# Layer-1 modulation of a two-layer diffusion trunk: from TensorE matmuls to sums on VectorE, ScalarE and GpSimd

## Chip, core and metric

One core of one Trainium2 chip. The metric is the device time of one execution of the whole program in microseconds, as the median of several runs.

## What is computed

A trunk of two layers over 256 latent tokens (x) and 256 context tokens (ctx), width 2048, in float32. Layer 0 runs neighbourhood attention (8 heads) beside latent attention (8 heads); layer 1 is a gated DeltaNet over both token sets. Each layer is steered by a modulation, and that is what the change is about:

```python
def adaln_params(cond, w_mod, b_mod):
    return jnp.split(jax.nn.silu(cond) @ w_mod + b_mod, 3, axis=-1)      # shift, scale, gate
def modulate(x, gain, shift, scale):
    return rmsnorm(x, gain) * (1 + scale) + shift
...
sh, sc, gt = adaln_params(c, w_mod, b_mod)              # for x
sh_c, sc_c, gt_c = adaln_params(c_ctx, w_mod, b_mod)    # for ctx
hx = modulate(x, norm, sh, sc) @ w_in
hc = modulate(ctx, norm, sh_c, sc_c) @ w_in
...
x = x + gt * y
if update_ctx:                                          # layer 0 only
    ctx = ctx + gt_c * y_c
```

For each layer two vectors of 2048 (one for x, one for ctx, the two "samples" of the change) go through a 2048 x 6144 matrix. The last layer does not update ctx, so its gate for ctx is never used.

## The kernel before

All activations lie feature-major: 128 features on the partitions, the 512 tokens (256 of x, 256 of ctx) along the free dimension. A dense product takes a weight tile of 128 x 1024, which ScalarE casts to a high part (whi, line 77) and VectorE completes with a low part (wlo = raw - whi, line 78); TensorE then runs three 128x512 matmuls per contraction tile (lines 90 to 92) into one of two mm tiles in PSUM. Weights come through SP's DMA queue into four raw buffers, whi and wlo have three buffers each.

The 6144 outputs of a modulation are cut into 12 chunks of 512: chunks 0 to 3 are the shift, 4 to 7 the scale, 8 to 11 the gate. A chunk reads 16 contraction tiles of 128x512, two to an mraw buffer (three buffers). There are two ways to compute one:

- `adaln` (TensorE, line 127): sixteen matmuls of four column groups into a PSUM tile pmod, a copy macc (line 133), four transposes pmt (line 136), and a reduction into the tile mod (line 138).
- `adaln_lanes` (lines 147 to 179): for each of the 16 contraction tiles and each of the two samples, VectorE adds tile times condition to a running sum lacc (lines 161 and 163), 32 instructions a chunk. Eight short matmuls pml with a column of ones (line 170) then sum over the partitions.

Both are generators; the work around them calls `steps` to take some steps of the one at hand, and a scheduler, which orders the instructions of every engine by its own estimate of time, settles the final order. Every engine runs its queue strictly in that order. The stages that matter:

- the first stage (layer 0's input products, with layer 0's shift and scale by `adaln`);
- the neighbourhood heads 0 to 6 (tiles qT, kT, vT, sp, pr, PT, po). Beside them run, as lanes, chunks 8 to 11 of layer 0 and chunks 0 and 1 of layer 1;
- the latent ranks (craw), head 7, the rope queries qr, and the latent heads, whose weights are ab_wb. Beside them run chunks 2, 3 and 8, and at the end chunk 9 of layer 1 by `adaln` on TensorE;
- the gated outputs gh and gl (lines 480 and 481), and the output projection (weights ab_wo), sixteen units, each closed by x1A and x1B (line 493). Beside them run chunks 4 to 7 of layer 1 as lanes;
- the turn into layer 1: the norm (ss, rs, dg, rb, lines 190 to 199), `modulate` (mh on VectorE, line 221; hh on ScalarE, line 222; hl on GpSimd, line 229, or on VectorE, line 224), and layer 1's first products. Here chunks 10 and 11 run by `adaln`;
- layer 1: keys, queries, inverses (GpSimd: rhs, line 711), then the scans and the output.

The attention of a head goes sp (TensorE) to mx (VectorE, line 372) to pr (ScalarE's exponential, line 375) to rc and pr again (VectorE, lines 377 and 378) to pt (TensorE) to PT (ScalarE line 340, VectorE line 341) to po (TensorE) to goA and goB (VectorE, line 388). goB of a head marks its end; the stretches of the prediction are cut at such instructions.

## Time and profile before

| | |
|---|---|
| median of 3 runs | 2585.1 us (2583.42 to 2586.82) |
| span of the profiled execution, first to last instruction | 2580.0 us |
| mean granted TensorE clock | 0.985 |
| TensorE busy | 97% |
| VectorE / ScalarE / GpSimd busy | 72% / 44% / 10% |
| bytes moved | 394.30 MB, 153 GB/s on average |

The profiled execution's own time is its span of 2580.0 us; the median of the timed runs is 5.1 us more, and the sums are made on the span. The profile calls TensorE PE (PEld is its weight load), VectorE DVE, ScalarE ACT, GpSimd POOL and SyncE SP. In a row of busy time by stage stand the stretch in us from the start, its length, the busy time and instruction count of each engine, the granted clock, the share of the DMA engines and GB/s; the same table for one tile or one line counts that tile's or line's instructions only. In a row of a tile stand minimum, median and maximum duration in ns, then the first and last start. In a row of the timeline stand start, duration, engine, line, operation, out<-in, shape, count, and in brackets idle time before it and what ended it. In a row of a group stand busy us, mean ns and idle time before. A matmul record lasts 0.39 us while the next one starts after 0.23 us.

### The profile page before, as it was taken

How to read it: one execution, taken by the hardware profiler on the slowest of the kernel's cores; microseconds unless marked ns; L12 is line 12 of the kernel's file. 1: busy time of each engine (PE TensorE's matmuls, PEld its weight loads, DVE VectorE, ACT ScalarE, POOL GpSimd, SP SyncE). 2: the span in 40 equal slices, each digit the busy share in tenths (PEclk: the TensorE clock that was granted, in tenths of full speed). 3: DMA queues.
4: the chain of work that ended last, by engine and by line, in shares of the span. 5: the costliest groups of instructions: out<-in, count | busy, mean ns of one | idle time of the engine just before them, and what ended most of it. 6: DMA issues, size and time to landing. Idle time of an engine off the chain costs nothing.

```text
span 2580.0 us, 43446 instructions
## 1 busy us (share of the span) xinstructions
PE 2499.2 (97%) x16586; PEld 2039.0 (79%) x16586; DVE 1852.2 (72%) x3543; ACT 1146.6 (44%) x2484; POOL 267.4 (10%) x261
## 2 busy tenths in 40 slices
PE   6999999999999999989999999999999999999998
PEld 4657888888767788768888889897777777777898
DVE  4544788773455687758999999987677777777754
ACT  4223323232333422377656655643444445445353
POOL 0000000000000000133212222310000000003000
PEclk9999999999999999999999999999999999999999
DMA  8872655532343376644454544563333433335454
GB/s 258 289 247 90 201 172 167 175 114 96 117 153 100 120 230 221 212 139 157 142 156 152 160 138 150 159 213 100 88 99 115 119 99 106 113 91 174 153 188 140
DMA packets 201810, 394.30 MB, mean 153 GB/s; under 512 B 68225, under 2 KB 109697, under 8 KB 201473
## 3 DMA queue, kind: packets, MB, share of 16 engines
q1 hardware_dynamic: 200448, 389.98, 47.9%
q8 instruction: 131, 2.15, 0.4%
q10 hardware_dynamic: 1152, 1.54, 0.2%
q14 instruction: 79, 0.64, 0.1%
HBM read 356.28 MB, written 35.13 MB: 152 GB/s over the span
## 4 chain that ended last, share of the span: by engine, by line
PE 79%; DVE 9%; issue 6%; DMA 3%; ACT 2%; SPq 0%; POOL 0%; DVEq 0%; POOLq 0%; ACTq 0%
PE mm L90 19%; PE mm L91 18%; PE mm L92 18%; PE pks L982 3%; PE pmod L127 3%; DVE wlo L78 2%; PE sp L348 2%; PE ptr L994 2%; DVE X L770 1%; DVE outer L768 1%; PE po L348 1%; PE pu L798 1%; DVE acc L561 1%; PE ptr L1027 1%; PE psu L1013 1%
## 5 line engine op out<-in xcount | busy, mean ns | idle before, releaser
L90 PE MATMUL mm<-hh,whi 128*128 128x512 f32 (+1 forms) x2784 | 988.5, 355 | 3.7 <-ACT t L636 2.2
L92 PE MATMUL mm<-hh,wlo 128*128 128x512 f32 (+1 forms) x2784 | 962.2, 346 | 8.7 <-DVE wlo L78 7.5
L91 PE MATMUL mm<-hl,whi 128*128 128x512 f32 (+1 forms) x2784 | 963.2, 346 | 0.0
L77 ACT CAST whi<-raw 128x1024 fp32r<-128x1024 f32 (+2 forms) x346 | 338.3, 979 | 668.4 <-PE mm L91 515.6
L90 PEld LDWEIGHTS mm<-hh,whi 128*128 128x128 f32 x2784 | 535.7, 192 | 113.8 <-issue 32.6
L92 PEld LDWEIGHTS mm<-hh,wlo 128*128 128x128 f32 x2784 | 535.4, 192 | 73.1 <-DVE wlo L78 9.4
L91 PEld LDWEIGHTS mm<-hl,whi 128*128 128x128 f32 x2784 | 536.0, 193 | 62.2 <-issue 8.4
L78 DVE TENSOR_TENSOR wlo<-raw,whi 128x1024 fp32r<-128x1024 f32 (+2 forms) x346 | 402.7, 1166 | 212.9 <-ACT whi L77 206.1
L163 DVE SCALAR_TENSOR_TENSOR lacc<-mraw,cond,lacc 128x512 f32<-128x512 f32 x300 | 208.8, 749 | 0.0
L561 DVE SCALAR_TENSOR_TENSOR acc<-cin,taps,acc 128x508 f32<-128x508 f32 (+3 forms) x256 | 196.1, 767 | 6.7 <-ACT acc L552 4.3
L1004 DVE SCALAR_TENSOR_TENSOR vl<-ptr,egm,vh 128x128 fp32r<-128x128 f32 x224 | 64.6, 346 | 98.3 <-ACT rf L1001 39.4
L711 POOL TENSOR_TENSOR rhs<-ghl,incl 128x512 fp32r<-128x512 f32 (+1 forms) x96 | 108.4, 1139 | 133.4 <-PE pd L713 114.2
L127 PE MATMUL pmod<-mraw,cond 128*32 128x512 f32 (+2 forms) x640 | 94.3, 501 | 23.2 <-DMA mraw<-ab_wm 18.6
L768 DVE SCALAR_TENSOR_TENSOR outer<-L,bv,X 128x31 f32<-128x31 f32 (+15 forms) x248 | 112.4, 453 | 4.7
L1088 DVE TENSOR_TENSOR wlo<-raw,whi 128x1024 fp32r<-128x1024 f32 x84 | 102.6, 1222 | 14.4 <-ACT whi L1080 13.8
L194 POOL TENSOR_TENSOR rs<-ms,half 128x4 f32<-128x4 f32 (+1 forms) x5 | 4.7, 947 | 985.1 <-DVE ms L192 985.1
L770 DVE TENSOR_TENSOR X<-X,outer 128x31 f32<-128x31 f32 (+15 forms) x248 | 101.7, 410 | 4.6
L575 ACT ACTIVATE ac<-acc 128x128 f32<-128x128 f32 x160 | 37.4, 300 | 146.0 <-DVE acc L561 146.0
L90 PE MATMUL mm<-gh,whi 128*128 128x512 f32 x256 | 99.9, 392 | 1.7 <-DVE x1B L493 1.7
L91 PE MATMUL mm<-gl,whi 128*128 128x512 f32 x256 | 99.9, 390 | 0.2 <-DVE gl L481 0.2
L92 PE MATMUL mm<-gh,wlo 128*128 128x512 f32 x256 | 99.7, 390 | 0.0
L998 ACT ACTIVATE vh<-ptr,egm 128x128 fp32r<-128x128 f32 x224 | 71.0, 373 | 56.6 <-PE ptr L994 54.6
(289 smaller groups left out, 3629.2 us busy)
## 6 DMA issues: line engine op xcount, KB each, us to landing
raw<-dn_w SPq DMA_DIRECT2D x194, 512.0 KB, 4.0
mraw<-dn_wm SPq DMA_DIRECT2D x96, 512.0 KB, 4.7
mraw<-ab_wm SPq DMA_DIRECT2D x88, 512.0 KB, 5.4
raw<-ab_w SPq DMA_DIRECT2D x66, 512.0 KB, 3.8
raw<-dn_wo SPq DMA_DIRECT2D x64, 512.0 KB, 3.7
raw<-ab_wo SPq DMA_DIRECT2D x32, 512.0 KB, 4.6
raw<-ab_w SPq DMA_DIRECT2D x32, 256.0 KB, 3.6
spt<-sp SPq DMA_DIRECT2D x64, 128.0 KB, 2.8
```

What stands on the lines that cost most here:

```text
L77: A.copy(hi[:, :m], raw[:, :m])
L78: V.tensor_tensor(lo[:, :m], raw[:, :m], hi[:, :m].bitcast(F32), op=ALU.subtract)
L90: PE.matmul(ps, wh[:, c], xh[:, k0 + k, sl], start=first and k == 0, stop=False)
L91: PE.matmul(ps, wh[:, c], xl[:, k0 + k, sl], start=False, stop=False)
L92: end = PE.matmul(ps, wl[:, c], xh[:, k0 + k, sl], start=False, stop=last and k == kt - 1)
L127: PE.matmul(pmod[32 * q:32 * q + 32, :m], cond[:, 4 * kg + q, :], raw[c // 1024][:, half + c % 1024:half + c % 1024 + m], start=kg == 0, s ...
L163: V.scalar_tensor_tensor(acc[:, s], raw[:, q], cond[:, k, s:s + 1], acc[:, s], op0=ALU.mult, op1=ALU.add)
L561: V.scalar_tensor_tensor(o3[:, :, i0:i1], p3[:, :, i0 + d:i1 + d], taps[:, ch, t:t + 1], o3[:, :, i0:i1], op0=ALU.mult, op1=ALU.add)
L711: P.tensor_tensor(rhs, ghl[i].bitcast(F32)[:, d, kh * 8:kh * 8 + 2 * n].unsqueeze(2).broadcast_to(sh), incl[:, c].unsqueeze(1).broadcast_t ...
L768: V.scalar_tensor_tensor(o, L[:, rows, k:k + 1].broadcast_to([128, n, m]), bv[:, k:k + 1], X[:, k:k + 1, cols].broadcast_to([128, n, m]), ...
L770: V.tensor_tensor(X[:, rows, cols], X[:, rows, cols], o, op=ALU.subtract)
L1088: V.tensor_tensor(w, raws[j], h.bitcast(F32), op=ALU.subtract)
```

## The change

After the first stage no chunk is computed by `adaln`: every later chunk goes through `adaln_lanes`, and that is rewritten.

- The sum of sample 0 stays on VectorE (16 instructions a chunk). For sample 1, ScalarE multiplies the tile by the condition, in place in the mraw buffer (after VectorE has read it), and GpSimd adds it to a second running sum. The first of them is written by ScalarE directly.
- The last four chunks of layer 1 (8 to 11, the gate) are made for sample 0 alone: `ns` is 1, VectorE takes the even contraction tiles, ScalarE and GpSimd the odd ones, and the closing matmuls add the two running sums.
- Chunks 2, 3 and 8 are stepped three at a time in the latent heads; chunk 9 leaves the end of the latent heads and chunks 10 and 11 leave the turn; 9, 10 and 11 follow 4 to 7 beside the output projection, two steps at a time.

```diff
     def adaln_lanes(l, ps, pm, tp, chunks, after=None):
         for ch in chunks:
-            acc = tp.tile([128, 2, 512], F32, name="lacc", tag="lacc", bufs=1)
+            ns = 1 if l == 1 and ch >= 8 else 2
+            acc = [tp.tile([128, 512], F32, name=f"lacc{i}", tag=f"lacc{i}", bufs=1) for i in range(2)]
...
-                        for s in range(2):
-                            if k == 0:
-                                V.tensor_scalar(acc[:, s], raw[:, q], cond[:, k, s:s + 1], None, op0=ALU.mult)
+                        for e in range(2):
+                            if ns == 1 and e != k % 2:
+                                continue
+                            c = cond[:, k, e * (ns - 1):e * (ns - 1) + 1]
+                            if e == 0 and k == 0:
+                                V.tensor_scalar(acc[e], raw[:, q], c, None, op0=ALU.mult)
+                            elif e == 0:
+                                V.scalar_tensor_tensor(acc[e], raw[:, q], c, acc[e], op0=ALU.mult, op1=ALU.add)
+                            elif k <= 2 - ns:
+                                A.activation(acc[e], raw[:, q], AF.Copy, scale=c)
                             else:
-                                V.scalar_tensor_tensor(acc[:, s], raw[:, q], cond[:, k, s:s + 1], acc[:, s],
-                                                       op0=ALU.mult, op1=ALU.add)
+                                A.activation(raw[:, q], raw[:, q], AF.Copy, scale=c)
+                                P.tensor_tensor(acc[e], acc[e], raw[:, q], op=ALU.add)
...
-                for s in range(2):
-                    PE.matmul(pt[:, j, s:s + 1], acc[:, s, j * 128:j * 128 + 128], ones[:, 0:1], start=True, stop=True)
+                for e in range(2):
+                    s = e * (ns - 1)
+                    PE.matmul(pt[:, j, s:s + 1], acc[e][:, j * 128:j * 128 + 128], ones[:, 0:1],
+                              start=ns == 2 or e == 0, stop=ns == 2 or e == 1)
...
-        ahead, pace = later(mr, ((0, range(8, 12), 1), (1, (0, 1), 1))), 1
+        ahead, pace = later(mr, ((0, range(8, 12)), (1, (0, 1)))), 1
...
-        ahead = later(mr, ((1, (2, 3, 8), 0),))
+        ahead = later(mr, ((1, (2, 3, 8)),))
...
-            steps(ahead, 1)
+            steps(ahead, 3)
...
-        steps(later(mr, ((1, (9,), 0),), last_mm))
...
-                ahead, pace = later(mr, ((1, (4, 5, 6, 7), 1),), last_mm), 1
+                ahead, pace = later(mr, ((1, (4, 5, 6, 7, 9, 10, 11)),), last_mm), 2
...
-        ahead = later(mr, ((1, (10, 11), 0),), last_mm)
...
-        steps(ahead)
```

How the scheduler then orders the engines, at the places of which the prediction speaks. First VectorE in the latent heads, the third head as its stream stands before: attention alone (vt, mx, PT, qT, kT), the reciprocal rc and the low parts wlo of the weights.

```order
L344 SCALAR_TENSOR_TENSOR qT<-mm,qT 128x512
L377 RECIPROCAL rc<-sm 128x1
L378 TENSOR_SCALAR pr<-pr,rc 128x256
L78 TENSOR_TENSOR wlo<-raw,whi 128x512
L341 TENSOR_TENSOR kT<-mm,kT 128x512
L341 TENSOR_TENSOR PT<-pt,PT 128x4x128
```

The same place now (line numbers of the changed kernel; lacc_7517 is VectorE's running sum of chunk 4):

```order
L352 SCALAR_TENSOR_TENSOR qT<-mm,qT 128x512
L386 TENSOR_SCALAR pr<-pr,rc 128x256
L78 TENSOR_TENSOR wlo<-raw,whi 128x512
L166 TENSOR_SCALAR lacc_7517<-mraw,cond 128x512
L349 TENSOR_TENSOR kT<-mm,kT 128x512
L184 TENSOR_TENSOR mod_84<-pml,vecs 128x4
L168 SCALAR_TENSOR_TENSOR lacc_7517<-mraw,cond,lacc_7517 128x512
L349 TENSOR_TENSOR PT<-pt,PT 128x4x128
L385 RECIPROCAL rc<-sm 128x1
L168 SCALAR_TENSOR_TENSOR lacc_7517<-mraw,cond,lacc_7517 128x512
L386 TENSOR_SCALAR pr<-pr,rc 128x256
L168 SCALAR_TENSOR_TENSOR lacc_7517<-mraw,cond,lacc_7517 128x512
```

Chunk 4, which ran beside the output projection, now stands among the latent heads. Between the end of head 7 of the neighbourhood and the end of the last latent head there are 80 lane sums on VectorE, 80 scalings on ScalarE and 75 adds on GpSimd, of chunks 2 to 6 and 8; 24 of the lane sums stand before the first latent head's end. Before there were 11 lane sums of chunk 4 in all this. In the neighbourhood heads 1 to 6 there are 74 lane sums and 70 adds, chunk by chunk at the same places as before; in the output projection 40 lane sums are left.

Second TensorE in the turn into layer 1, before: the norm's sums ss, then chunk 10 (pmod) around the broadcast rb and the first products of layer 1 (mm from hh and hl).

```order
L190 MATMUL ss<-ones,sq 128x1
L127 MATMUL pmod<-mraw,cond 32x512 x6
L199 MATMUL rb<-dg,ones 128x128 x4
L127 MATMUL pmod<-mraw,cond 32x512 x2
L90 MATMUL mm<-hh,whi 128x512 x2
L127 MATMUL pmod<-mraw,cond 32x512 x4
L91 MATMUL mm<-hl,whi 128x512
```

The same place now:

```order
L201 MATMUL ss<-ones,sq 128x1
L210 MATMUL rb<-dg,ones 128x128 x4
L90 MATMUL mm<-hh,whi 128x512 x2
L91 MATMUL mm<-hl,whi 128x512
L92 MATMUL mm<-hh,wlo 128x512
```

Nothing stands between the norm and the products any more; their closing matmuls pml are ahead of the norm, in the output projection.

More of the change, by code (lines that the diff above doesn't have):

```diff
@@ L307, in later @@
         def later(pool, parts, after=None):
-            for l, chunks, lanes in parts:
-                if lanes:
-                    yield from adaln_lanes(l, ps, "pm", pool, chunks, after)
-                else:
-                    yield from adaln(l, ps, ("pm", "pm"), pool, [(4 * ch, 4) for ch in chunks], after=after)
-        ahead, pace = later(mr, ((0, range(8, 12), 1), (1, (0, 1), 1))), 1
+            for l, chunks in parts:
+                yield from adaln_lanes(l, ps, "pm", pool, chunks, after)
+        ahead, pace = later(mr, ((0, range(8, 12)), (1, (0, 1)))), 1
         def unit(xh, xl, src=None):
```

6 lines of the change are left out of this document (3 added, 3 removed).

## The prediction

> **What bounds the kernel now.** I read the page first, then the table of busy time by stage, then single tiles in each stage. The page shows one nearly full engine, and a GpSimd that has almost nothing to do:
>
> ```profile
> PE 2499.2 (97%) x16586; PEld 2039.0 (79%) x16586; DVE 1852.2 (72%) x3543; ACT 1146.6 (44%) x2484; POOL 267.4 (10%) x261
> PE 79%; DVE 9%; issue 6%; DMA 3%; ACT 2%; SPq 0%; POOL 0%; DVEq 0%; POOLq 0%; ACTq 0%
> ```
>
> The change touches four stretches: the neighbourhood heads, the latent heads, the output projection, and the turn into layer 1. The last two rows split the latent stretch: its first head with the rope queries, and heads 1 to 6.
>
> ```profile
> core 0: us, PE busy (x) PEld busy (x) DVE busy (x) ACT busy (x) POOL busy (x), PEclk, DMA share, GB/s
> 327.30:572.20 244.90, 244.90 (x1235) 207.24 (x1234) 192.75 (x327) 75.07 (x133) 0.00 (x0) 1.00 0.49 160
> 709.50:905.90 196.40, 192.11 (x980) 137.23 (x980) 115.90 (x254) 79.88 (x184) 0.00 (x0) 1.00 0.38 127
> 905.90:1069.80 163.90, 162.06 (x744) 134.67 (x742) 132.98 (x204) 41.56 (x62) 0.00 (x0) 1.00 0.68 221
> 1069.80:1116.00 46.20, 43.96 (x197) 24.92 (x196) 28.28 (x59) 27.24 (x62) 18.38 (x16) 0.93 0.61 204
> 709.50:758.70 49.20, 46.73 (x224) 30.08 (x224) 25.10 (x51) 17.39 (x34) 0.00 (x0) 1.00 0.49 165
> 758.70:880.20 121.50, 120.36 (x633) 86.98 (x632) 66.33 (x144) 56.40 (x137) 0.00 (x0) 1.00 0.33 107
> ```
>
> TensorE ends every stretch last; VectorE is 79% busy in the first (192.75 of 244.90), 59% in the latent heads, 81% in the output projection; GpSimd does nothing before the turn. So time leaves only where TensorE loses work and VectorE, now the second engine, does not become the first.
>
> **What goes from TensorE.** Six chunks of layer 1 (2, 3, 8, 9, 10, 11) were matmuls. What they and their transposes cost inside the stretches, and the five lane chunks' closing products of the first stretch:
>
> ```profile
> 709.50:905.90 196.40, 20.47 (x108) 3.19 (x108) 2.77 (x4) 1.00 0.38 127
> 1069.80:1116.00 46.20, 15.15 (x64) 2.18 (x64) 1.38 (x2) 0.93 0.61 204
> ```
> ```profile
> 709.50:905.90 196.40, 2.51 (x16) 1.83 (x16) 0.76 (x4) 1.00 0.38 127
> 1069.80:1116.00 46.20, 0.65 (x5) 0.55 (x5) 0.19 (x1) 0.93 0.61 204
> ```
> ```profile
> 327.30:572.20 244.90, 9.43 (x80) 10.03 (x80) 0.79 (x5) 1.00 0.49 160
> ```
> ```profile
> 700.48 1.88 PE L127 MATMUL pmod<-mraw,cond 128*32 128x512 f32 x8
> ...
> 707.67 1.05 PE L127 MATMUL pmod<-mraw,cond 128*32 128x512 f32 x4 [0.24 <-DMA mraw<-dn_wm]
> ```
>
> Removed: 20.47 + 2.51 in the latent stretch, 15.15 + 0.65 in the turn, and four groups just ahead of 709.5 (one of 1.88 and three of 1.05, 5.0). A lane chunk closes with 9.43 / 5 = 1.9. By the new order six chunks now close in the latent stretch or at its end: 2, 3, 8 and also 4, 5 and 6, which used to run beside the output projection. TensorE's latent stretch becomes 196.4 - 23.0 + 6 x 1.9 = 184.8, or 180.5 if its present idle time (196.40 - 192.11 = 4.3) goes too. A forecast from TensorE alone would be about 12 to 16 there.
>
> **What comes to VectorE there.** In a run of lane sums the next starts before the last one's record ends:
>
> ```profile
> 915.67 4.06 DVE L163 SCALAR_TENSOR_TENSOR lacc<-mraw,cond,lacc 128x512 f32<-128x512 f32 x6
> ```
> ```profile
> L163 DVE SCALAR_TENSOR_TENSOR lacc<-mraw,cond,lacc 128x512 f32<-128x512 f32 x120 | 84.5, 747 | 0.0
> L78 DVE TENSOR_TENSOR wlo<-raw,whi 128x1024 fp32r<-128x1024 f32 x36 | 44.0, 1223 | 30.0 <-ACT whi L77 29.8
> ```
> ```profile
> 327.30:572.20 244.90, 9.43 (x80) 10.03 (x80) 101.80 (x149) 1.00 0.49 160
> 709.50:905.90 196.40, 0.00 (x0) 0.00 (x0) 7.15 (x11) 1.00 0.38 127
> 905.90:1069.80 163.90, 6.44 (x57) 6.76 (x57) 79.30 (x118) 1.00 0.68 221
> ```
>
> Six take 4.06, the last one 0.75 of it, so the step is 3.31 / 5 = 0.66. The new order has 80 of them in the latent stretch where 11 ran. VectorE's own work: 115.9 - 7.15 (old lanes) - 2.8 (copies of pmod) + 80 x 0.66 = 158.8. That alone still fits under 184.8.
>
> **What GpSimd's adds do to it.** The add has no row of its own, but a subtraction of the same shape has, and the turn shows both engines meeting:
>
> ```profile
> L229 POOL TENSOR_TENSOR hl<-mh,hh x22: 1277/1298/2287, 30.7 to 1108.2; 128x512 fp32r<-128x512 f32 x22
> ```
> ```profile
> 1083.26 1.30 POOL L229 TENSOR_TENSOR hl<-mh,hh 128x512 fp32r<-128x512 f32 x1 [0.70 <-ACT mh L227]
> ...
> 1098.52 1.58 POOL L229 TENSOR_TENSOR hl<-mh,hh 128x512 fp32r<-128x512 f32 x1 [1.72 <-ACT mh L227]
> ```
> ```profile
> 1083.55 1.30 DVE L224 SCALAR_TENSOR_TENSOR hl<-mh,mod,hh 128x256 fp32r<-128x256 f32 x1
> ...
> 1098.46 0.48 DVE L224 SCALAR_TENSOR_TENSOR hl<-mh,mod,hh 128x256 fp32r<-128x256 f32 x1
> ```
> ```profile
> L224 DVE SCALAR_TENSOR_TENSOR hl<-mh,mod,hh x20: 473/483/1542, 67.3 to 1104.5; 128x256 fp32r<-128x256 f32 x20
> ```
> ```profile
> L78 DVE TENSOR_TENSOR wlo<-raw,whi x36: 1214/1224/1229, 363.9 to 594.9; 128x1024 fp32r<-128x1024 f32 x36
> ```
> ```profile
> L221 DVE SCALAR_TENSOR_TENSOR mh<-x1A,Am,rb x16: 468/476/481, 1078.6 to 1105.9; 128x256 f32<-128x256 f32 x16
> ```
>
> VectorE's 0.48 us operation, begun 0.29 into a GpSimd one, took 1.30 and ended 0.29 after it; begun 0.06 ahead, it kept 0.48 and GpSimd's took 1.58. They take turns, and GpSimd holds VectorE up for some 1.15 of its 1.30. Where GpSimd is idle (36 wlo in the neighbourhood stretch) the spread is 15 ns; mh in the turn, which reads one of its tensors (rb) from PSUM, never grows although GpSimd runs beside it. So only VectorE's instructions with both tensors in SBUF are stopped. The Trainium skill, "SBUF — State Buffer", section "Who interferes with whom", says the same and calls it an exclusive lock held for the whole instruction; by that, 1.30 and not 1.15 would be held, and the sum below would end 8 us later. The skill's "Perfetto Trace Analysis", section "Optimizing Scalar/DVE Operations", warns that offloading between these two engines might not help, because of the same port; both speak against this change.
>
> All 80 lane sums, the wlo and the gl have both tensors in SBUF. The order has 75 GpSimd adds in the latent stretch. If every hold stopped VectorE fully: 158.8 + 75 x 1.15 = 245. If all fell on its other instructions or idle time: 158.8, and TensorE's 184.8 ends last. I take two thirds of a hold, 0.76, because the order puts a both-in-SBUF instruction second or third after nearly every lane sum: 158.8 + 57 = 216. Thus VectorE becomes the bound, and the stretch goes from 196.4 to 216, **+20**. The row of the first head carries most of it: 24 sums there instead of none over 49.2.
>
> ScalarE gets 80 scalings. Nearest row, a cast of the same width (an estimate for them):
>
> ```profile
> L77 ACT CAST whi<-raw 128x512 fp32r<-128x512 f32 x24 | 14.9, 619 | 61.9 <-PE mm L91 40.9 <-DMA raw<-ab_w 9.8 <-PE pz L91 9.6
> ```
>
> 79.88 + 80 x 0.62 = 129 of 196, hidden. But each scaling overwrites what VectorE must have read, and behind it in ScalarE's queue stand the exponentials and whi; each add frees the mraw that SP's queue waits for, and behind that wait stand raw loads of ab_wb. The raw tiles reach two heads ahead, so I price both at nothing; that cover gone is the second rival.
>
> **The other stretches.** Neighbourhood: chunk order unchanged, 192.75 - 101.8 + 74 x 0.66 + 70 x 0.76 = 193, as full as before; I take +3, between 0 and 12. Ahead of the latent stretch, with eight lane sums in its place: -4 of the 5.0. Output projection: VectorE falls from 133 to 133 - 79 + 40 x 0.66 = 80, four chunks close as before, and TensorE at 162.06 of 163.9 has nothing to give: 0. In the turn the pmod matmuls stood in front of what mattered:
>
> ```profile
> 1074.84 0.87 DVE L198 TENSOR_SCALAR dg<-ident,rs 128x128 f32<-128x128 f32 x4 [1.19 <-POOL rs L194]
> ...
> 1115.20 0.69 DVE L133 COPY macc<-pmod 128x512 f32<-128x512 f32 x1 [8.42 <-PE pmod L127]
> ```
> ```profile
> 1076.93 1.60 PE L199 MATMUL rb<-dg,ones 128*128 128x128 f32 x8
> ```
>
> The first dg was done about 1075.2, rb began at 1076.93. Of 15.8 freed, ScalarE's 27.24 and VectorE's 28.28 of modulation and casts keep a part; -8, between -4 and -13. Layer 1 has the same work: 0.
>
> **Sum.** +3 - 4 + 20 + 0 - 8 = +11 on the profiled 2580.0; the median of the runs lies 5.1 above that, so 2580.0 + 11 + 5.1 = 2596.
>
> **Rivals.** *The holds are hidden (faster).* If under 26 us of them fall on VectorE's path (184.8 - 158.8, 0.35 an add), TensorE still ends the latent stretch: -14, -4, -8, neighbourhood 0, -26 in all, 2559. For it: VectorE is idle for two fifths of that stretch now, and many of its present instructions there (mx, PT, vt, qT, kT, go) read a PSUM tile and so run on beside an add. Against: the lane sums themselves fill that idle time, and each add follows a lane sum with more of them behind it. *The four queues lock into one loop (much slower).* VectorE waits for holds, ScalarE for VectorE, GpSimd for ScalarE, SP for GpSimd, and every hold counts: 245 - 196.4 = +49, neighbourhood +10, -4, -8, so +47, 2632. *Gain and loss cancel*, which is also what remains if the change only moves work: latent stretch some 209, +13, the rest -9; 2589, within 0.2% (5.2 us, about what a measurement of this kernel tells from no change).
>
> **Chances.** Forecast, slower by 6 to 28 us: 0.36, its own range 2591 to 2613. Hidden holds: 0.31. Loop: 0.16. Cancelled: 0.17. Faster 0.31, same 0.17, slower 0.52. The range goes from the hidden holds at their bounds (-16, -4, -13: 2552) to the loop at its own (+49, +12, -4, -4: 2638), with about a tenth left out at each end.
>
> **What would show it.** In the new profile: wlo and lane sums in the neighbourhood and latent stretches with a spread up to 1.2 us above their minimum, GpSimd about 100 busy in the latent stretch, VectorE over 95% and TensorE idle there on wlo, PT or vt. Wrong, if TensorE stays full there, if the adds take far from 1.3, or if the loss lies in a stretch other than the latent one.

## The result and the profile after

The changed kernel takes 2647.5 us (median of 4 runs, 2644.99 to 2657.76) against 2584.6 us for the kernel before in the same session: a ratio of 1.0256, with a 95% interval of 1.0234 to 1.0277. It is slower by 63 us; 11 were forecast. The profiled execution has a span of 2643.7 us, and the sums below are made on spans (2580.0 before).

The page of the changed kernel: TensorE's busy time has not fallen, although it has less work, VectorE carries twice its share of the chain that ended last, and GpSimd's add, which the prediction had to price by a subtraction, has a row of its own.

```profile
PE 2502.4 (95%) x16466; PEld 2057.1 (78%) x16466; DVE 1937.4 (73%) x3435; ACT 1289.2 (49%) x2704; POOL 600.9 (23%) x469
PE 63%; DVE 18%; issue 9%; DMA 5%; ACT 4%; POOL 1%; SPq 0%; DVEq 0%; POOLq 0%; ACTq 0%
...
L173 POOL TENSOR_TENSOR lacc<-lacc,mraw 128x512 f32<-128x512 f32 x208 | 335.0, 1610 | 491.2 <-ACT mraw L172 238.5
...
L168 DVE SCALAR_TENSOR_TENSOR lacc<-mraw,cond,lacc 128x512 f32<-128x512 f32 x208 | 238.7, 1148 | 25.8 <-DMA mraw<-dn_wm 19.0
...
L172 ACT ACTIVATE mraw<-mraw,cond 128x512 f32<-128x512 f32 x208 | 149.1, 724 | 203.2 <-DVE lacc L168 120.0
```

An add takes 1.61 us on average, a lane sum on VectorE 1.15 instead of 0.75. Busy time by stage of the changed kernel, in the columns used before: the neighbourhood heads, the ranks with head 7, the latent heads, the output projection, and the first latent head alone.

```profile
329.90:597.90 268.00, 249.73 (x1226) 206.16 (x1225) 200.16 (x254) 126.23 (x209) 121.41 (x73) 0.99 0.46 148
597.90:742.90 145.00, 137.58 (x633) 113.40 (x631) 62.75 (x93) 47.82 (x72) 10.84 (x9) 0.97 0.31 98
742.90:970.90 228.00, 196.36 (x942) 152.54 (x942) 207.10 (x323) 131.86 (x265) 115.85 (x76) 0.91 0.45 143
970.90:1147.10 176.20, 171.29 (x758) 142.08 (x758) 109.54 (x125) 67.43 (x101) 58.19 (x36) 0.95 0.64 206
742.90:808.70 65.80, 51.89 (x211) 38.86 (x212) 60.08 (x77) 35.95 (x62) 37.56 (x24) 0.82 0.43 140
```

Against the rows of before: neighbourhood heads 244.9 to 268.0 (+23.1), ranks 137.3 to 145.0 (+7.7), latent heads 196.4 to 228.0 (+31.6, of which the first head +16.6), output projection 163.5 to 176.2 (+12.7). What follows the last x1B takes 14.0 less (10.0 of it in the turn, up to the first sigmoid of layer 1, and 4.0 in layer 1), what precedes the first goB 2.7 more. TensorE, which had stood still for nothing in the neighbourhood heads (244.90 of 244.90), now waits 18.3 us there, and 31.6 in the latent heads. The granted clock, 1.00 in all four stretches before, is down to 0.91 in the latent heads and 0.82 in the first of them.

### The profile page after: what moved, and what is told of

Read it like the earlier page. It is cut to its first block, busy times and chain, and to the rows that moved or that the text cites. A ratio compares the mean times of both kernels' runs of the same rounds, so it can differ in the third digit from the quotient of the medians.

```text
span 2643.7 us, 43867 instructions
## 1 busy us (share of the span) xinstructions
PE 2502.4 (95%) x16466; PEld 2057.1 (78%) x16466; DVE 1937.4 (73%) x3435; ACT 1289.2 (49%) x2704; POOL 600.9 (23%) x469
## 4 chain that ended last, share of the span: by engine, by line
PE 63%; DVE 18%; issue 9%; DMA 5%; ACT 4%; POOL 1%; SPq 0%; DVEq 0%; POOLq 0%; ACTq 0%
PE mm L90 15%; PE mm L92 14%; PE mm L91 14%; DVE lacc L168 4%; DVE wlo L78 4%; PE pks L987 3%; DMA mraw<-dn_wm 2%; PE ptr L999 2%; PE pmod L127 2%; DVE acc L566 2%; PE sp L356 1%; DMA mraw<-ab_wm 1%; DVE X L775 1%; DVE outer L773 1%; PE pu L803 1%
## 5 line engine op out<-in xcount | busy, mean ns | idle before, releaser
L78 DVE TENSOR_TENSOR wlo<-raw,whi 128x1024 fp32r<-128x1024 f32 (+2 forms) x346 | 431.6, 1249 | 263.8 <-ACT whi L77 255.6
L173 POOL TENSOR_TENSOR lacc<-lacc,mraw 128x512 f32<-128x512 f32 x208 | 335.0, 1610 | 491.2 <-ACT mraw L172 238.5
L168 DVE SCALAR_TENSOR_TENSOR lacc<-mraw,cond,lacc 128x512 f32<-128x512 f32 x208 | 238.7, 1148 | 25.8 <-DMA mraw<-dn_wm 19.0
L172 ACT ACTIVATE mraw<-mraw,cond 128x512 f32<-128x512 f32 x208 | 149.1, 724 | 203.2 <-DVE lacc L168 120.0
```

What stands on the lines that cost most here:

```text
L78: V.tensor_tensor(lo[:, :m], raw[:, :m], hi[:, :m].bitcast(F32), op=ALU.subtract)
L168: V.scalar_tensor_tensor(acc[e], raw[:, q], c, acc[e], op0=ALU.mult, op1=ALU.add)
L172: A.activation(raw[:, q], raw[:, q], AF.Copy, scale=c)
L173: P.tensor_tensor(acc[e], acc[e], raw[:, q], op=ALU.add)
```

## The experiments

The table holds every run: the median and its ratio to the kernel before, run beside it on the same chip, and the length of the stretches in the profiled execution, cut at the same instructions (first goB, goB of heads 6, 7 and the last, last x1B).

| kernel | median us | ratio (95%) | neighbourhood | ranks | latent | output | after it |
|---|---|---|---|---|---|---|---|
| before | 2584.6 | 1 | 245.0 | 137.3 | 196.4 | 163.4 | 1510.6 |
| changed | 2647.5 | 1.0256 (1.0234-1.0277) | 268.0 | 144.9 | 228.0 | 176.2 | 1496.6 |
| GpSimd writes, does not read | 2583.3 | 1.0007 (0.9995-1.0020) | 242.5 | 142.3 | 202.8 | 167.8 | 1496.8 |
| no scaling on ScalarE | 2670.0 | 1.0346 (1.0330-1.0361) | 268.8 | 148.5 | 244.6 | 171.0 | 1501.1 |
| VectorE alone | 2598.2 | 1.0068 (1.0053-1.0083) | 245.0 | 141.2 | 213.9 | 169.8 | 1498.4 |
| offload alone, nothing moved | 2613.3 | 1.0125 (1.0108-1.0142) | 267.5 | 142.3 | 196.9 | 170.1 | 1505.9 |
| half an add | 2600.4 | 1.0076 (1.0054-1.0097) | 245.3 | 143.9 | 216.4 | 170.2 | 1492.0 |
| gates beside the latent heads | 2579.9 | 0.9988 (0.9977-1.0000) | 245.0 | 138.3 | 202.5 | 166.1 | 1494.7 |
| gates beside the output projection | 2583.0 | 1.0003 (0.9993-1.0014) | 245.0 | 137.8 | 207.4 | 165.9 | 1499.3 |
| six chunks left out, loads stay | 2573.0 | 0.9963 (0.9947-0.9979) | 245.0 | 136.4 | 190.6 | 165.0 | 1509.6 |
| six chunks left out, loads too | 2554.7 | 0.9897 (0.9881-0.9912) | 245.0 | 134.3 | 183.6 | 165.4 | 1498.9 |
| two gates beside the neighbourhood | 2574.1 | 0.9968 (0.9956-0.9981) | 241.4 | 140.6 | 197.0 | 163.4 | 1499.2 |
| four gates beside the neighbourhood | 2591.8 | 1.0039 (1.0025-1.0052) | 245.5 | 162.9 | 187.7 | 163.4 | 1499.3 |
| two early, a third beside the output | 2571.3 | 0.9959 (0.9946-0.9973) | 241.0 | 141.5 | 195.4 | 166.2 | 1495.0 |

A cut lies at an instruction of VectorE, and TensorE's work can cross it. Of the matmuls of the dense products, which start 0.23 us apart, 877 stand in the neighbourhood heads and 479 in the ranks before, 869 and 497 in the changed kernel and in the offload alone, 866 and 495 where GpSimd writes, 855 and 494 with two gates beside the neighbourhood. So some 4 us of what the ranks gain or lose in these kernels, and the 242.5 and 241.4 of the neighbourhood, are work on the other side of a cut.

Three theories stood. A: the add of GpSimd and the sums of VectorE take turns at SBUF, and VectorE, longer, is late for TensorE. B: ScalarE's scaling, which waits for VectorE and for a transfer, holds up the casts and exponentials behind it. C: the moved chunks burden the latent heads, whoever adds.

### GpSimd writes instead of adding

```diff
-                                P.tensor_tensor(acc[e], acc[e], raw[:, q], op=ALU.add)
+                                P.memset(raw[:, q], 0.0)
```

> The changed kernel with GpSimd's add replaced by a write of zeros into the same half of the mraw buffer: GpSimd still comes after ScalarE's scaling and still frees the buffer, but reads no tensor and adds nothing (left out: sample 1's sum beyond its first tile, so the modulation of ctx, or half of a one-sample chunk, is incomplete). Theory A (the turns of VectorE and GpSimd at SBUF are the loss): VectorE's lane sums and wlo fall back to their own length (0.66 to 0.75 and 1.22 us), neighbourhood heads from 268.0 back to 245-248 us, latent heads from 228.0 to 190-200, output projection from 176.2 to 163-167, the whole about 2575 to 2600. Theory B (the loss is ScalarE's in-place scaling that waits for VectorE and for the mraw transfer with whi, exponentials and vT behind it, whatever GpSimd does): neighbourhood stays at 260 or more, output projection near 176, the whole above 2620. A part of each: in between, and the table by stretch tells which stretch belongs to which.

The whole loss is gone: 2583.3 is no different from the kernel before. This kernel, by stage (neighbourhood, latent heads, output), and its lane sums in the neighbourhood beside the writes:

```profile
326.70:569.20 242.50, 242.25 (x1223) 204.84 (x1222) 150.11 (x254) 124.69 (x206) 37.37 (x70) 1.00 0.48 160
711.50:914.30 202.80, 192.38 (x956) 152.63 (x956) 158.11 (x325) 131.61 (x266) 39.94 (x75) 0.94 0.49 160
914.30:1082.10 167.80, 164.58 (x744) 136.43 (x744) 83.60 (x122) 66.75 (x100) 18.93 (x36) 0.98 0.67 217
```
```profile
L168 DVE SCALAR_TENSOR_TENSOR lacc<-mraw,cond,lacc x70: 730/752/754, 326.0 to 553.5; 128x512 f32<-128x512 f32 x70
L173 POOL MEMSET mraw<- x70: 524/527/835, 327.6 to 555.0; 128x512 f32 x70
```

The same two lines of the changed kernel in its neighbourhood heads, where GpSimd reads:

```profile
L168 DVE SCALAR_TENSOR_TENSOR lacc<-mraw,cond,lacc x71: 725/1111/1779, 328.3 to 585.0; 128x512 f32<-128x512 f32 x71
L173 POOL TENSOR_TENSOR lacc<-lacc,mraw x73: 1263/1621/2162, 329.5 to 587.7; 128x512 f32<-128x512 f32 x73
```

Minimum, median and maximum of a lane sum are 730, 752 and 754 ns beside writes, 725, 1111 and 1779 beside adds. A holds and B falls: ScalarE's scalings and the order of the queues were all still there, and its waits for lane sums too, though shorter (21.8 us in the neighbourhood instead of 57.6, below). The write is also shorter than the add, 0.53 against 1.62 us, and so frees the mraw buffer sooner; but VectorE waited no less for the loads into mraw (16.0 us in the neighbourhood here, 9.5 in the changed kernel), so late buffers are not what was gained there. The Trainium skill says in "SBUF — State Buffer", section "Who interferes with whom", that a VectorE instruction with two SBUF inputs contends with a GpSimd instruction that reads SBUF and not with one that only writes it; these rows agree on both counts.

A mean price per add can be read from VectorE's busy time with and without the reads: neighbourhood (200.16 - 150.11) / 73 = 0.69 us, latent (207.10 - 158.11) / 76 = 0.64, output (109.54 - 83.60) / 36 = 0.72. The prediction took 0.76.

But a second thing shows here. Without any hold VectorE is busy 158.1 of the latent stretch, just what the prediction worked out (158.8), and yet that stretch takes 202.8 and not TensorE's 184.8.

### No scaling on ScalarE

```diff
-                                A.activation(raw[:, q], raw[:, q], AF.Copy, scale=c)
                                 P.tensor_tensor(acc[e], acc[e], raw[:, q], op=ALU.add)
```

> The changed kernel without ScalarE's scaling of each tile; GpSimd adds the unscaled tile (left out: sample 1's condition factor, beyond the first tile of a chunk). GpSimd's adds stay, 205 or so. Theory A (turns at SBUF): the lane sums and wlo stay long (lane sum median about 0.88, wlo up to 2.3 us), most of the loss stays, neighbourhood 260 or more, latent heads 215 or more, the whole above 2625. Theory B (ScalarE's queue): ScalarE waits for no lane sum any more, neighbourhood back to 245-250, output projection to 163-168, the whole about 2590 to 2610. If both are needed (VectorE held up by GpSimd, ScalarE by VectorE, TensorE by ScalarE), this and the run with the write of zeros each give back most of it.

It became slower still, 2670.0. With the scaling gone an add is ready as soon as its tile has landed, and more of them collide: the median lane sum is 1652 ns instead of 878. The trace shows how a stretch in which VectorE is by no means full can lose time. In this kernel, one place of the neighbourhood heads, on GpSimd, VectorE, ScalarE and TensorE:

```profile
384.72 18.55 POOL L172 TENSOR_TENSOR lacc<-lacc,mraw 128x512 f32<-128x512 f32 x11 [29.14 <-ACT lacc L170]
```
```profile
386.33 10.18 DVE L168 SCALAR_TENSOR_TENSOR lacc<-mraw,cond,lacc 128x512 f32<-128x512 f32 x6
396.43 2.30 DVE L78 TENSOR_TENSOR wlo<-raw,whi 128x1024 fp32r<-128x1024 f32 x1
398.65 6.74 DVE L168 SCALAR_TENSOR_TENSOR lacc<-mraw,cond,lacc 128x512 f32<-128x512 f32 x5
...
407.97 0.67 DVE L379 TENSOR_REDUCE mx<-sp 128x1 f32<-128x512 f32 x1
```
```profile
408.67 0.69 ACT L382 ACTIVATE pr<-sp,mx 128x512 f32<-128x512 f32 x1 [12.50 <-DVE mx L379]
```
```profile
409.50 1.01 PE L355 MATMUL sp<-kT,qT 128*128 128x256 f32 x3 [6.27 <-ACT pr L382]
```

Read it downwards. Eleven adds stand back to back, 18.55 / 11 = 1.69 us each; VectorE's lane sums alternate with them, six in 10.18, 1.70 each, where the kernel before did six in 4.06. Behind them in VectorE's queue stands mx, which is late; ScalarE's exponential has waited 12.50 for it, and TensorE 6.27 for the exponential. VectorE's busy share does not show this: its queue is strictly in order, and a burst of sums that takes 2.5 times as long delays whatever stands behind it.

In the changed kernel the same alternation reaches TensorE by another way too. A place in its neighbourhood heads, GpSimd and then VectorE (the next wlo also grows, 1.2 to 2.20), and below what ScalarE and TensorE waited for in that stretch (us in total, times, longest):

```profile
387.67 12.88 POOL L173 TENSOR_TENSOR lacc<-lacc,mraw 128x512 f32<-128x512 f32 x7
388.17 2.20 DVE L78 TENSOR_TENSOR wlo<-raw,whi 128x1024 fp32r<-128x1024 f32 x1
390.30 6.89 DVE L168 SCALAR_TENSOR_TENSOR lacc<-mraw,cond,lacc 128x512 f32<-128x512 f32 x4
```
```profile
ACT mraw L172 <- DVE lacc L168: 57.6, 36, 3.3
ACT pr L383 <- DVE mx L380: 10.7, 8, 2.1
PE pv L362 <- ACT vT L400: 6.7, 2, 3.3
```
```profile
PE pt L389 <- DVE pr L386: 2.9, 3, 1.6
PE sp L356 <- ACT pr L383: 2.6, 3, 1.2
```

ScalarE waits 57.6 us for lane sums, with vT and the exponentials behind it; without the scaling its exponentials waited 56.3 us for mx instead of 10.7. So B describes a real path, but as one of two by which VectorE's delay travels, not as a cause: take the scaling away and the delay goes by mx; take the read away and both are gone.

### VectorE alone, at the change's places

```diff
-                            if e == 0 and k == 0:
+                            if k <= (e if ns == 1 else 0):
                                 V.tensor_scalar(acc[e], raw[:, q], c, None, op0=ALU.mult)
-                            elif e == 0:
+                            else:
                                 V.scalar_tensor_tensor(acc[e], raw[:, q], c, acc[e], op0=ALU.mult, op1=ALU.add)
-                            elif k <= 2 - ns:
-                                A.activation(acc[e], raw[:, q], AF.Copy, scale=c)
-                            else:
-                                A.activation(raw[:, q], raw[:, q], AF.Copy, scale=c)
-                                P.tensor_tensor(acc[e], acc[e], raw[:, q], op=ALU.add)
```

> The changed kernel with all sums on VectorE, at the change's places and with the last gates for one sample alone; ScalarE and GpSimd take no part. VectorE has about 150 sums of 0.66 us in the latent heads, with its other work there of 106: about 205 busy. If only the placement beside the latent heads costs (theory C): latent heads 205 to 215, neighbourhood 245, output projection about 164, turn -8 to -10, the whole 2580 to 2600. Theory A or B, that the work of GpSimd and ScalarE is the loss: the whole below 2585, that is at or under the kernel before, and neighbourhood and output projection exactly as before. If the whole is above 2620 the offload is innocent.

All sums on one engine, twice as many on VectorE, and it is some 49 us faster than the shared version. Neighbourhood and latent heads:

```profile
328.90:573.90 245.00, 245.00 (x1235) 207.25 (x1234) 192.68 (x327) 75.12 (x133) 0.00 (x0) 1.00 0.49 160
715.10:929.00 213.90, 194.47 (x940) 152.08 (x940) 195.54 (x391) 80.77 (x185) 0.00 (x0) 0.93 0.44 144
```

The neighbourhood is what it was. But the latent heads still lose 17.5, and the whole 18: C is true for a part of the loss, without any turns of two engines.

### The offload alone, nothing moved

The lanes function of the change in the kernel before, whose plan stays (2, 3, 8, 9, 10 and 11 of layer 1 on TensorE):

```diff
-                        for s in range(2):
...
+                        for e in range(2):
...
+                                A.activation(raw[:, q], raw[:, q], AF.Copy, scale=c)
+                                P.tensor_tensor(acc[e], acc[e], raw[:, q], op=ALU.add)
```

> The kernel before with nothing changed but the way a lane chunk is computed: sample 0 on VectorE, sample 1 on ScalarE and GpSimd. Chunks 2, 3, 8, 9, 10 and 11 of layer 1 stay on TensorE, so nothing is moved into the latent heads or out of the turn. If the offload costs wherever it stands (A or B): neighbourhood +20 to +25 as in the changed kernel, output projection +8 to +15, latent heads 0 to +5 (its few lane sums), turn 0, the whole 2612 to 2632. If the loss needs the moved chunks (C): all stretches within 5 of the kernel before, the whole about 2585.

```profile
330.00:597.50 267.50, 249.66 (x1226) 206.33 (x1226) 201.73 (x254) 126.13 (x209) 121.12 (x73) 0.99 0.45 148
739.80:936.70 196.90, 193.77 (x984) 138.16 (x984) 117.39 (x250) 83.92 (x190) 7.27 (x5) 1.00 0.38 124
```

The neighbourhood's loss is there to half a microsecond (267.5 beside 268.0), the latent stretch is untouched, the output projection loses 6.7 (8 to 15 expected). The offload costs wherever its adds stand.

### Half an add

```diff
-                                P.tensor_tensor(acc[e], acc[e], raw[:, q], op=ALU.add)
+                                P.tensor_tensor(acc[e][:, :256], acc[e][:, :256], raw[:, q, :256], op=ALU.add)
```

> The changed kernel with GpSimd's add cut to the first 256 of its 512 columns; ScalarE still scales the whole tile, and order and queues stay (left out: the other half of sample 1's sums). The first run with a write of zeros in place of the add gave the whole loss back, so what is open is whether the loss goes with the length of the hold. If it does: add about 0.65 to 0.75 instead of 1.61, neighbourhood 252 to 260 (half of the 23 lost), latent heads 212 to 220, the whole 2605 to 2622. If any add costs, however short, since it breaks VectorE's run of overlapping sums: neighbourhood 262 or more, the whole above 2630. If short holds hide completely: neighbourhood 245, the whole below 2592.

```profile
327.90:573.20 245.30, 244.06 (x1228) 205.44 (x1227) 166.00 (x254) 125.40 (x208) 73.18 (x73) 1.00 0.49 161
717.00:933.50 216.50, 197.04 (x956) 153.49 (x956) 176.99 (x325) 132.41 (x267) 67.24 (x75) 0.93 0.46 152
```
```profile
L168 DVE SCALAR_TENSOR_TENSOR lacc<-mraw,cond,lacc x208: 723/752/1306, 280.8 to 1088.9; 128x512 f32<-128x512 f32 x104
L173 POOL TENSOR_TENSOR lacc<-lacc,mraw x208: 722/842/1824, 282.4 to 1089.7; 128x256 f32<-128x256 f32 x104
```

None of the three expectations holds for the whole. VectorE's price per add falls to (166.00 - 150.11) / 73 = 0.22, a third of 0.69 for half the columns, and in the neighbourhood the loss is gone (245.3), while in the latent heads about half is left (216.4, between 202.8 and 228.0). The loss is no fixed price per add: the neighbourhood, where TensorE had no gap before, bears delays of this size, and the latent heads do not.

### What the removal could bring at all

In the first of two leave-outs the six chunks' loads stay and of each chunk's matmuls eight of 32 columns; in the second the loads are gone too, and the loads of chunks 4 to 7 are held where they were:

```diff
-        ahead = later(mr, ((1, (2, 3, 8), 0),))
+        ahead = iter(())
...
-        steps(later(mr, ((1, (9,), 0),), last_mm))
...
-                ahead, pace = later(mr, ((1, (4, 5, 6, 7), 1),), last_mm), 1
+                ahead, pace = later(mr, ((1, (4, 5, 6, 7), 1),), xd), 1
...
-        ahead = later(mr, ((1, (10, 11), 0),), last_mm)
```

> The kernel before with the work of chunks 2, 3, 8, 9, 10 and 11 of layer 1 left out: their loads stay, of 64 matmuls of 512 columns a chunk keeps 8 of 32 columns, and its transposes and reduction are gone (left out: these six chunks of the modulation). Nothing comes in their place on any engine, so this is the most that any move of them away from TensorE can bring. Theory that TensorE's work alone sets these stretches: latent heads 196.4 - 23 = 173 (169 if its idle time goes too), ahead of it -5, turn -16, the whole about 2535 to 2540. Theory that the matmuls of the modulation stand in gaps of TensorE and that beyond a point it waits for the attention's chain and its granted clock falls: latent heads 182 to 192 at a clock of 0.94 to 0.98, turn -12, the whole 2550 to 2565.

> As the leave-out before it, but the loads of the six chunks (24 MB) are gone too, with the small matmuls that waited for them (6.6 us in the latent heads there, after which the granted clock fell to 0.5 for some 10 us); the loads of chunks 4 to 7 are held behind the first residual's, so that their sums stay beside the output projection. Left out: chunks 2, 3, 8, 9, 10, 11 of layer 1, for which a constant stands. If those waits were what kept the first leave-out from its 40 us: latent heads 175 to 181, turn 30 to 36, the whole 2540 to 2552. If TensorE is held by the attention's chain and the turn's own work: latent heads 185 or more, turn 37 to 40 as in every run without matmuls of the modulation there, the whole 2558 to 2570.

The first gave 2573.0, above both expectations, because it kept something that costs: its small matmuls wait for their loads (latent heads, TensorE), and behind three such waits in a row the clock is 0.50. In the turn they wait 6.7 us more, and that is most of why the two leave-outs differ by 10.7 after the last x1B:

```profile
PE pmod L127 <- DMA mraw<-dn_wm: 6.6, 7, 1.5
```
```profile
861.00:866.00 5.00, 2.61 (x20) 2.06 (x19) 2.19 (x5) 5.00 (x16) 0.00 (x0) 1.00 0.96 314
866.00:871.00 5.00, 3.54 (x18) 2.67 (x19) 1.31 (x4) 2.99 (x11) 0.00 (x0) 0.71 0.82 283
871.00:876.00 5.00, 5.00 (x20) 4.06 (x20) 3.28 (x10) 1.64 (x4) 0.00 (x0) 0.50 0.40 153
```

The second, which came out between its two expectations, is the clean ceiling: 2554.7 us, 26 under the kernel before (ratio 0.9897, 0.9881 to 0.9912), with nothing put in place of 44 us of TensorE's work (23.0, 5.0 and 15.8). Its latent heads:

```profile
706.90:890.50 183.60, 175.31 (x860) 136.37 (x860) 112.10 (x243) 79.44 (x185) 0.00 (x0) 0.97 0.18 59
```

So 23.0 us less of TensorE's work make the latent heads 12.8 shorter, and not 23.0. An account of the latent heads follows. TensorE's work there at full clock is 192.11 - 20.47 - 2.51 = 169.1 without the six chunks, and the closing matmuls pml, 10.3 to 12.3 by their rows in each kernel, come on top. What the busy time has above that is the slower clock (the rows' clocks, 0.97, 0.94, 0.93 and 0.91 times the busy times, give the work back within 2 us):

| kernel | work | slower clock | idle | stretch |
|---|---|---|---|---|
| before | 192.1 | 0.0 | 4.3 | 196.4 |
| left out, loads too | 169.1 | 6.2 | 8.3 | 183.6 |
| GpSimd writes, does not read | 181.4 | 11.0 | 10.4 | 202.8 |
| VectorE alone | 179.4 | 15.1 | 19.4 | 213.9 |
| changed | 179.5 | 16.9 | 31.6 | 228.0 |

TensorE did get rid of its work, as predicted. It then waits the more, the more sums stand in VectorE's queue and the longer they take, and its clock is lower where it waits. What it waits for in the changed kernel's latent heads, the three longest in total:

```profile
PE pp L442 <- ACT rope L440: 8.4, 3, 4.5
PE sp L356 <- DVE kT L349: 6.2, 2, 4.3
PE pml L180 <- DVE lacc L168: 6.2, 2, 5.3
```

The first is for the rope queries, the second for a step of the attention's chain (kT, vt, qT, pr and PT come to 15.7 together), the third for the last sum of a chunk, which its closing matmuls need.

### Versions without the offload

Five versions take from the change only the gates for one sample, on VectorE alone (16 sums a chunk), and try places for them. In the first all four stand in the latent heads, and 2 and 3 stay on TensorE; in the second 9, 10 and 11 stand behind 4 to 7:

```diff
-        ahead = later(mr, ((1, (2, 3, 8), 0),))
+        ahead = later(mr, ((1, (2, 3), 0), (1, (8, 9, 10, 11), 1)))
...
```
```diff
-                ahead, pace = later(mr, ((1, (4, 5, 6, 7), 1),), last_mm), 1
+                ahead, pace = later(mr, ((1, (4, 5, 6, 7, 9, 10, 11), 1),), last_mm), 2
...
```

> The kernel before with three things taken from the change and not the offload: the gate chunks 8 to 11 of layer 1 for sample 0 alone, as lanes on VectorE (16 sums of 0.66 a chunk) beside the latent heads 2 to 7, chunks 10 and 11 out of the turn; chunks 2 and 3 stay on TensorE in the first latent heads, 4 to 7 beside the output projection as before. Theory of the filler (chunks 2 and 3 fill TensorE's gaps in the first latent head, and without them TensorE idles and its granted clock falls): first latent head about 49 at a clock of 1.00, as before; latent heads 188 to 196, output projection 163.5, turn 33 to 38 instead of 47.5; the whole 2562 to 2572. If VectorE's sums beside the attention cost by themselves, as in the run with all sums on VectorE (+17 there for some 150 sums): 64 sums cost some +7, latent heads about 203, and the whole is 2570 to 2580.

> The kernel before with chunks 9, 10 and 11 of layer 1 for sample 0 alone as lanes on VectorE behind chunks 4 to 7, whose first sums then stand beside the last latent heads; 2, 3 and 8 stay on TensorE. Latent heads 190 to 198 (chunk 9's matmuls gone, some 40 sums and two closings come in), output projection 163 to 167 (VectorE about 80 to 90% busy), turn 33 to 38; the whole 2562 to 2575. If VectorE beside the output projection is late with its low parts wlo, output projection 170 or more and the whole as before.

```profile
711.20:913.80 202.60, 190.20 (x944) 142.33 (x944) 160.63 (x331) 79.64 (x185) 0.00 (x0) 0.97 0.52 173
711.20:762.80 51.60, 48.28 (x233) 31.38 (x234) 29.32 (x60) 17.80 (x36) 0.00 (x0) 1.00 0.55 186
```

The first head keeps its clock of 1.00 with chunks 2 and 3 on TensorE, as the filler theory has it, but that theory's total does not come: the latent heads lose 6, although two chunks' matmuls left them (the other expectation said some +7). The trace has 89 lane sums there instead of 11: the gates' 64, and more of chunk 4 than before. Of the 16 and 11 us gained after the last x1B most is given back: 2579.9 and 2583.0, no change for the second, whose latent heads took 207.4 (190 to 198 expected).

In the next two the gates stand beside the neighbourhood heads, where VectorE alone cost nothing: chunks 10 and 11, then all four.

```diff
-        ahead, pace = later(mr, ((0, range(8, 12), 1), (1, (0, 1), 1))), 1
+        ahead, pace = later(mr, ((0, range(8, 12), 1), (1, (0, 1) + (10, 11), 1))), (1, 2)
...
```

> The kernel before with chunks 10 and 11 of layer 1 for sample 0 alone (16 sums a chunk on VectorE) taken out of the turn and run beside the neighbourhood heads, behind the six chunks that stand there; three steps a unit instead of two. 2, 3, 8 and 9 stay on TensorE. VectorE in the neighbourhood 193 + 32 x 0.66 = 214 of 245, TensorE gets two closings there: neighbourhood 245 to 250; latent heads and output projection as before; turn and what follows -14 to -16 (as in the run with the gates beside the latent heads). The whole 2566 to 2573. If VectorE's sums delay the attention there too: neighbourhood 255 or more, and the whole as before.

> As the run before it, with chunks 8 and 9 there too (four gates beside the neighbourhood heads; 2 and 3 stay on TensorE, 4 to 7 are held beside the output projection by issuing their loads behind the first residual's). VectorE in the neighbourhood 193 + 64 x 0.66 = 235 of 245: 246 to 258. Latent heads without two chunks' matmuls: 180 to 184 if TensorE alone sets them, 188 to 194 if it then waits for the attention's chain. Turn -14 to -16. The whole 2553 to 2568.

Two gates are nearly free there: VectorE at 209 of 241.5, the clock at 1.00, and 2574.1 in all, 7 under the kernel before. The 241.5 is no gain, since work crossed the cut; head 7 ends at 712.0 us instead of 709.5, and the two closings are 2.1 of that. The first row is the neighbourhood of the two-gate version; the second is the stretch behind it in the four-gate version, and what TensorE waited for there:

```profile
330.00:571.50 241.50, 241.50 (x1230) 204.68 (x1229) 209.42 (x355) 75.17 (x132) 0.00 (x0) 1.00 0.58 192
```
```profile
575.90:738.80 162.90, 140.57 (x652) 113.50 (x654) 68.01 (x106) 42.94 (x66) 2.02 (x2) 0.93 0.35 116
```
```profile
PE pml L171 <- DVE lacc L164: 20.1, 2, 17.6
```

Four are too many: two chunks are not finished when head 6 ends, and TensorE, in order, waits 20.1 us at their closing matmuls. The latent heads win 8.8, the ranks lose 25.6.

The last version keeps the two and puts chunk 9 behind 4 to 7:

> The version with two gates beside the neighbourhood heads, and chunk 9 for sample 0 alone as a lane on VectorE behind chunks 4 to 7 beside the output projection (loads held there), instead of on TensorE at the end of the latent heads. Latent heads 188 to 191 instead of 197 (chunk 9's matmuls and its waits for loads gone), output projection 163.4 to 167 (VectorE 143 of 163 busy), the rest as in the version with two gates: 2563 to 2571. If TensorE only waits for something else at the end of the latent heads, or the output projection gives it back: the same as with two gates, 2572 to 2577.

```diff
-        steps(later(mr, ((1, (9,), 0),), last_mm))
...
-                ahead, pace = later(mr, ((1, (4, 5, 6, 7), 1),), last_mm), (1, 1)
+                ahead, pace = later(mr, ((1, (4, 5, 6, 7, 9), 1),), xd), (1, 2)
```

2571.3 us, ratio 0.9959 (0.9946 to 0.9973): faster than the kernel before by 9 us and, by the two ratios, than the changed one by some 77; the expectation for the better case ended at 2571. The latent heads came to 195.4 and not to 188 to 191: chunk 9 is gone, but the clock there is 0.97 instead of 1.00. From the two-gate version it cannot be told apart.

## Why the prediction was wrong

The sign was right, and so was the hold of VectorE by GpSimd. What failed is how busy time was turned into time: each stretch was priced as the larger of TensorE's and VectorE's sums, and delays on an engine that is not full were put at nothing or next to it. So 64 us were lost on the spans and not 11. By its steps:

- **TensorE's removal** was counted whole in the latent heads, 23.0, and brought 12.8 in the clean leave-out; idle time and a slower clock took the rest. That "184.8, or 180.5" stands near the 183.6 measured there is chance: it holds 11.4 of closing products that the leave-out does not have. -4 ahead of it (-3.0) and -8 in the turn (-9.2) held. It is chance too that the rival in which all holds are hidden was 26 us faster and the leave-out is 26 faster: the rival has the sums in it, and the run without the reads, nearest to it, was 1 faster by its span.
- **The hold** was right in size: 0.76 an add was taken, 0.64 to 0.72 measured, and VectorE's 158.8 without holds was 158.1. The adds themselves averaged 1.61 and not 1.3.
- **The step that failed first** is "Neighbourhood: ... as full as before; I take +3, between 0 and 12". VectorE came to 200 (193 predicted) of a stretch that grew by 23.1. That VectorE was no fuller was taken to mean that it was no later. More than half of what the stretches lost, 43.5 beside 31.6, lies outside the latent heads, and the prediction had named that as a sign of being wrong. The lane sums run in bursts, and a burst at 1.70 a sum instead of 0.66 delays mx, pr and the scalings behind it. The prediction had 0.66 in its hand and the turns in its hand, and spread their product over the stretch.
- **The latent stretch** was forecast as the larger of two engines' sums, 216, and took 228.0. VectorE's 207.1 was under the forecast, and 91% of the stretch where over 95% was named as the sign; the other 21 are time in which neither is the bound, and "That alone still fits under 184.8" fell with the write of zeros: both engines fit, and the stretch took 202.8. Of the +31.6 in the stretch, 25.2 came with GpSimd's reads (228.0 - 202.8).
- **"ScalarE ... hidden", queues "priced at nothing"**: the cover was gone (ScalarE 57.6 us waiting for lane sums), but where GpSimd does not read, the 21.8 us of such waits that are left cost nothing (242.5). The second rival named this loop and put +10 on the neighbourhood.
- **The output projection**, "0", lost 12.7, though VectorE was only 110 of 176 busy. The runs give 4.4 with the write of zeros and 6.7 with the offload alone at the old place. TensorE's own records take 171.29 at a clock of 0.95. The trace shows where: the clock is 0.50 from 970.9 to 981.2, at the seam with the latent heads, and for 3.4 us behind each of two places at which the closings of a chunk wait for its last sums (3.7 us together). No run tried this by itself.
- **The ranks**, forecast at -4, lost 7.7. The write of zeros and the offload alone lost 5.0 there too, the second without a lane sum in the stretch and with its matmuls of the modulation still there; some 4 us in each are the matmuls that crossed the cut. In the changed kernel TensorE also waits 5.9 us for head 7's own attention (PT, pr, rc), at a clock of 0.97, and 5.7 of pmod are gone. What the lane sums beside head 7 cost by themselves was not tried.
- **Layer 1**, "0", gained 4.0. The runs do not agree there: the offload alone, whose chunks 10 and 11 stay in the turn, is 10.1 shorter than the kernel before, and the run without the scaling, in which they leave it, 0.5 longer. So the 4.0 cannot be put down to the change.

The sum in its own terms: the leave-out's -25; +24 from adding up elsewhere without a read (loads, closings, sums and scalings between the attention's steps, slower clock: the run with writes, -1 in all); +65 from the adds of GpSimd in place of writes. The last is one edit, and the lane sums and the half add say that it is the reads; the middle one is a difference of two kernels and is not divided further than the table does.

## What to carry to other kernels

Before work is moved off the bounding engine, leave it out once: here 44 us of matmuls were worth 26, and that was the budget for everything that came in their place. The busy share of the receiving engine says how much more it can hold, not how late its next instruction is; on an engine that works strictly in order, look at what stands behind a burst and how long the burst becomes when another engine takes turns with it. Nor does the receiver's idle time say where to put the work: with VectorE alone, the neighbourhood heads, 79% full and with no gap on TensorE, took 32 more sums for 2.5 us, and the latent heads, with 80 us idle on VectorE, lost 6 us to 78 more, although two chunks' matmuls had left them. Why the two differ was not tried by itself.

## What the hardware showed that was not expected

TensorE's granted clock fell to half when it had waited in several short pieces, and stayed there while it worked again. The changed kernel at the end of head 7 and in the first latent head, in slices of 6 us:

```profile
728.00:734.00 6.00, 2.79 (x16) 2.06 (x14) 4.50 (x9) 3.92 (x10) 1.67 (x2) 1.00 0.67 256
734.00:740.00 6.00, 3.44 (x15) 2.40 (x15) 6.00 (x9) 2.64 (x6) 4.40 (x4) 0.61 0.52 175
740.00:746.00 6.00, 2.50 (x8) 2.03 (x8) 5.90 (x10) 2.91 (x6) 3.96 (x4) 0.50 0.40 124
746.00:752.00 6.00, 4.91 (x12) 3.86 (x13) 5.96 (x6) 2.48 (x4) 5.76 (x4) 0.50 0.40 128
```

The mean of 0.61 in the second slice puts the fall from 1.00 to 0.50 some 1.3 us into it, at about 735.3. The two longest of TensorE's waits ahead of it, from its timeline:

```profile
732.44 0.38 PE L356 MATMUL po<-PT,vt 128*128 128x256 f32 x1 [2.04 <-ACT PT L348]
734.59 2.11 PE L356 MATMUL po<-PT,vt 128*128 128x256 f32 x11 [1.76 <-DVE PT L349]
```

No single wait before the fall is longer than 2.04 us, and in the second slice TensorE is still busy 3.44 of 6. A longer one, 4.47 us for the rope queries' pp, comes only behind the fall and ends at 747.1; from there to the end of the last slice TensorE works without a gap at half the clock. The Trainium skill, "TensorE: Matmul & The Clock Gate", section "Part 1: The HAM clock gate (the "warmup" mystery)", has the two states, full and half, and a change to half after an idle window of about 3.4 us; the two states are seen here (0.50), but the clock fell with no single wait that long. In the latent heads of the four kernels without the six chunks' matmuls, the slower clock cost 0.5 to 1.1 us for each us of waiting (6.2 to 8.3, 11.0 to 10.4, 15.1 to 19.4, 16.9 to 31.6): an idle microsecond of TensorE was worth more than itself there. It is no fixed price, for the kernel before waited 4.3 us in these heads and kept its clock. And matmuls that fill such gaps cost less than their length: of the modulation's the first latent head held 9.1 us of busy time (8.41 of pmod, 0.66 of pmt), and without them and their loads it was 3.3 shorter (45.9 instead of 49.2).
